# Weight remainders on VectorE during the scan's inverse, a rotation copy on GpSimd, and an order edge for the RWKV output

## The chip, the cores and the metric

The kernel runs on one core of one Trainium2 chip. The metric is the device time of one execution in microseconds (us). Engines are named as the profile names them: PE is TensorE's matmul and PEld its weight load, DVE is VectorE, ACT is ScalarE, POOL is GpSimd, SP is the engine that issues most DMAs. L265 is line 265 of the kernel before.

## The reference, cut to what matters

Two layers act on 512 latent and 256 context tokens of width 1024. Each layer normalises its input, projects it with one wide matrix, feeds three groups of heads, and projects their joint output back:

```python
p_l = split_projection(h @ w_in)          # latent, 4352 columns
p_c = split_projection(hc @ w_in)         # context
y_rwkv = rwkv_mixer(...)                  # 4 heads of 64, forward and backward in time
y_conv = short_conv_mixer(...)            # width 3
y_attn = diff_attention_mixer(...)        # 4 heads, rotary positions on q and k
x = x + gate * rms_norm(concat(y_rwkv, y_conv, y_attn) @ w_out, post_g)
```

RWKV is a recurrence, once per direction. The attention part rotates q and k of the latent tokens before the scores:

```python
S = S * w_t + (S @ a_t) b_t + v_t k_t;  y_t = S @ r_t
rotate: concat([x1 * cos - x2 * sin, x2 * cos + x1 * sin])
RWKV readout: y = group_norm(y_fwd + y_bwd) * ln_g + ln_b + bonus * v, times silu(z)
```

## The kernel before

**Numbers in two parts.** Most large matmuls run in a reduced-precision 32-bit format (F32R), so an operand is held as a rounded high part and a remainder ("low part"), and three products are summed: high by high, high of the weight by low of the activation, low of the weight by high of the activation. `split` (L247 to L269) does it for each 128x512 piece of a weight matrix: a DMA on SP's queue brings the raw piece (`wraw`, two buffers), ACT casts it (`whi`, L265), and one subtraction (`wlo`, L268) makes the low part. `whi` and `wlo` have three buffers each. The variable `eng` chooses who subtracts. A running count would alternate GpSimd and VectorE, but with `pool_only` the choice is always GpSimd, and the projections that fill the scan all pass `pool_only`.

**Filler.** The projections of the conv group, the gates, and attention's q, k and v are Python generators that emit a few matmuls at each step. `fill(us)` advances them by a number of microseconds of matmul work. They are spread through the RWKV scan, so that PE has independent work while the recurrence waits.

**The scan.** `rwkv_scan` handles the 768 tokens in three blocks b = 0, 1, 2 of 256 tokens for each direction d = 0, 1; a block has four chunks of 64 tokens. For a block, `rwkv_stage1` builds small matrices R (matmul `s`, masked by DVE), `rwkv_diag` collects diagonal blocks D, and `rwkv_inverse` inverts triangular matrices. The inverse begins with 28 dependent DVE steps on tiny operands (tiles `invt` and `Acc`, L118 in the profile since every DVE operation is recorded at the line of the wrapper `Vec`); between them the function `hook` emits filler. Four groups of small matmuls (`mg`) follow, each behind `fill` of 3 to 4 us. While a block is inverted, `adv` also advances `rwkv_prep` of the next block, which uses ACT, DVE and POOL (tiles `ld`, `Lc`, `E`, `Ei`, `km`, `x1`, `ar`, `bk`).

Then four steps p = 0 to 3 run one after the other, each a serial chain: PE `ch<-zu,R`; DVE copies to `gs`; PE `ch<-gs,XT`; two copies to `zu` on ACT (L968) and two on DVE; PE `ch<-zu,R` again; and DVE adds `pz`, which POOL (L947) made from the previous `zu`. The outputs `Y` are copied by ACT (L991) or added by DVE.

**Rotation of q and k.** For each of four heads h, `qk` in `attn_proj` projects q (i = 0) and k (i = 1). ACT evicts them from PSUM into `t` (tile `qkr`, L1118); four DMAs bring the half-swapped copy `sw` (tile `qks`, L1123). Then `sw` is multiplied by the sine on POOL (L1124), `t` by the cosine (L1125) and the two are added (L1126); the sum is cast into `sw` as the high part by ACT (L1127), the low part is `t` minus `sw` (L1128), and both go to DRAM. The three operations at L1125, L1126 and L1128 are on DVE for the heads in `QV = (2, 3)` and on POOL for heads 0 and 1.

**RWKV output.** `rwkv_out` normalises `Y`: in layer 0 first the four context chunks, then the eight latent chunks; in layer 1 the latent chunks alone. It loads v into `Vs`, and POOL multiplies it by the bonus and adds a bias (L1019, L1021). DVE reduces the means (`mu`), subtracts them, and computes a variance from ACT's squares (`gnsq`), a reciprocal root, two products and a sum. PE transposes the result (`yT`) and DVE multiplies it by the gate into `yr`. `Vs`, `gnsq` and the scan's `ar` share two buffers (tag `wk`).

**What sets the order.** Each engine runs its own queue in order. The queues are laid out at compile time by a list scheduler: it takes the program order as priority and places an instruction when its own model of the times says that it is ready. An edge of class `NoSync` given by `add_manual_dep` makes the scheduler place one instruction behind another without a semaphore. A wait that is longer on the chip than in the model holds everything behind it on that queue.

Of the kernel before, what the change touches and what calls it, by code (L numbers as in the profile page):

```python
# [11 lines left out]
F32R = mybir.dt.float32r  # L12
I32 = mybir.dt.int32
AF = mybir.ActivationFunctionType
ALU = mybir.AluOpType
AX = mybir.AxisListType
PSUM = bass.MemoryType.PSUM

P = 128
# [7 lines left out]
HD = 64  # L27
# [38 lines left out]
QV = (2,3)  # L66
# [40 lines left out]
def build(tc, A):  # L107
    nc = tc.nc
    ctx = ExitStack()
    S, G = nc.scalar, nc.gpsimd  # L110
# [17 lines left out]
    V = Vec()  # L128
# [63 lines left out]
    def small(n, tag, pool=None, bufs=2):  # L192
        return (pool or sm).tile([P, n], F32, tag=tag, bufs=bufs, name=tag)
# [55 lines left out]
    def split(src_ap, pool=wp, tag="w", out_tag=None, pool_only=False, nr=WR, nh=WH, out_pool=None):  # L249
        if lin.get("raw") and tag == "w":  # L250
            raw = lin["raw"].tile([P, 512], F32, tag="oraw", bufs=OB, name="wraw")
        else:
            raw = pool.tile([P, 512], F32, tag=tag + "raw", bufs=nr, name=tag + "raw")
        i = nc.sync.dma_start(out=raw, in_=src_ap)
        if lin.get("wafter"):
            tc.add_manual_dep(i.ins, lin["wafter"], mybir.DependencyInfo(
                mybir.DependencyClass.NoSync, mybir.DependencyReason.DATA), reason="order")
            lin["wafter"] = None
        if out_tag is None:
            hi = pool.tile([P, 512], F32R, tag=tag + "hi", bufs=nh, name=tag + "hi")  # L260
            lo = pool.tile([P, 512], F32R, tag=tag + "lo", bufs=nh, name=tag + "lo")
        else:
            hi = out_pool.tile([P, 512], F32R, name=out_tag + "hi")
            lo = out_pool.tile([P, 512], F32R, name=out_tag + "lo")
        S.copy(hi, raw)  # L265
        wcount[0] += 1
        eng = G if wcount[0] % 2 == (tag != "m") or pool_only else V
        eng.tensor_tensor(out=lo, in0=raw, in1=hi.bitcast(F32), op=ALU.subtract)  # L268
        return hi, lo  # L269

# [564 lines left out]
    def rwkv_scan(l, st, rw, lat, cx):  # L835
# [38 lines left out]
        for b in range(3):  # L874
# [21 lines left out]
            def adv(k):  # L896
                while pq and k:
                    try:
                        next(pq[0])
                        k -= 1  # L900
                    except StopIteration:
                        pq.pop(0)
# [8 lines left out]
            def hook(i):  # L911
                fill(F["i"] if b < 2 else F["i2"])
                if i >= H0 and i % HD_ == 0:
                    adv(1)

            rwkv_inverse(od, D, Bm, MS, I32, rw, XT, hook, adv)
            adv(AP)
            fill(F["m2"])
            for p in range(4):
# [19 lines left out]
                for d in range(2):  # L939
                    gs[d] = rw.tile([P, 2, HD], F32, tag="gs", bufs=2, name="gs")  # L940
                    cp = V.tensor_copy(gs[d], pv[d][:, 0])
                if not end:
                    for d in range(2):
                        pz[d] = rw.tile([P, 2, HD], F32, tag="pz", bufs=2, name="pz")
                        for h in range(2):
                            hr = slice(h * 64, h * 64 + 64)
                            G.tensor_tensor(out=pz[d][hr], in0=zu[d][hr, :, h, :],  # L947
                                            in1=prepd[d][1][hr, :, cc[d][1]].unsqueeze(2).to_broadcast([64, 2, HD]),
                                            op=ALU.mult)
# [49 lines left out]
    def rwkv_out(l, st, yr, rw):  # L999
        n = NL if l == L - 1 else NT  # L1000
        zr = rw.tile([P, 2, NT], F32, tag="kkn", name="zr")
        nc.sync.dma_start(out=zr[:, :, :n], in_=zrd[l].rearrange("a p t -> p a t")[:, :, :n])
        Y = st["Y"]
        lng = rw.tile([P, 2, 2, HD], F32, tag="lng", name="lng")
        for h in range(2):
            nc.scalar.dma_start(out=lng[h * 64:h * 64 + 64].rearrange("p a b v -> p (a b v)"),
                                in_=A["lngb"][l, h:h + 1, :].to_broadcast([64, 256]))
        for c0, nch in ((0, 8),) if l == L - 1 else ((8, 4), (0, 8)):
            nu = nch * 2
            Yu = Y[:, c0:c0 + nch].rearrange("p c a v -> p (c a) v")  # L1010
            bon = st["bon"][:, 2 * c0:2 * c0 + nu]
            Vs = rw.tile([P, 8, 2, HD], F32, tag="wk", bufs=WK, name="Vs")
            for h in range(2):
                for hp in range(2):
                    o = hp * P + h * 64
                    nc.sync.dma_start(out=Vs[h * 64:h * 64 + 64, 0:nch, hp, :],
                                      in_=vd[l][c0 * 64:(c0 + nch) * 64, o:o + 64].rearrange("(c t) v -> t c v", t=64))
            Vu = Vs[:, :nch].rearrange("p c a v -> p (c a) v")
            G.tensor_tensor(out=Vu, in0=Vu, in1=bon.unsqueeze(2).to_broadcast([P, nu, HD]), op=ALU.mult)  # L1019
            for hp in range(2):  # L1020
                G.tensor_tensor(out=Vs[:, :nch, hp], in0=Vs[:, :nch, hp],  # L1021
                                in1=lng[:, 1, hp].unsqueeze(1).to_broadcast([P, nch, HD]), op=ALU.add)
            mu = small(24, "mu")
            V.tensor_reduce(out=mu[:, :nu], in_=Yu, axis=AX.X, op=ALU.add)
            V.tensor_scalar_mul(mu[:, :nu], mu[:, :nu], -1.0 / HD)
            V.tensor_tensor(out=Yu, in0=Yu, in1=mu[:, :nu].unsqueeze(2).to_broadcast([P, nu, HD]), op=ALU.add)
            sq = rw.tile([P, 24, HD], F32, tag="wk", bufs=WK, name="gnsq")
            S.activation(sq[:, :nu], Yu, AF.Square)
            var = small(24, "var")
            V.tensor_reduce(out=var[:, :nu], in_=sq[:, :nu], axis=AX.X, op=ALU.add)  # L1030
            V.tensor_scalar(out=var[:, :nu], in0=var[:, :nu], scalar1=1.0 / HD, scalar2=GN_EPS,
                            op0=ALU.mult, op1=ALU.add)
            rs = small(24, "gnrs")
            rsqrt(var[:, :nu], nu, rs[:, :nu])
            V.tensor_tensor(out=Yu, in0=Yu, in1=rs[:, :nu].unsqueeze(2).to_broadcast([P, nu, HD]), op=ALU.mult)
            for hp in range(2):
                yh = Y[:, c0:c0 + nch, hp]
                V.tensor_tensor(out=yh, in0=yh, in1=lng[:, 0, hp].unsqueeze(1).to_broadcast([P, nch, HD]), op=ALU.mult)
                V.tensor_tensor(out=yh, in0=yh, in1=Vs[:, :nch, hp], op=ALU.add)
                fill(F["o"] if hp == 0 else F["o2"])  # L1040
                lin["next"] = MG & 64
                pb = psalt("yT")
                for c in range(nch):
                    for h in range(2):
                        hr = slice(h * 64, h * 64 + 64)
                        T.matmul(pb[hr, c * 64:c * 64 + 64], Y[hr, c0 + c, hp, :], ident[hr, hr], start=True, stop=True,
                                 tile_position=(h * 64, h * 64))
                n = nch * 64
                ts_ = slice(c0 * 64, c0 * 64 + n)
                V.tensor_tensor(out=yr[:, hp, ts_], in0=pb[:, :n], in1=zr[:, hp, ts_], op=ALU.mult)  # L1050
# [54 lines left out]
    def attn_proj(l, lat, cx):  # L1105
# [8 lines left out]
        def qk(h, fk=()):  # L1114
            for i in range(2):
                t, sw = fst("qkr"), fst("qks")
                yield from proj_ch(l, lat, cx if i else cxx,
                                   lambda o, c, nn: S.mul(t[:, c:c + nn], o, 1.0 if i else 0.125), fk=fk)  # L1118
                nn = NT if i else n
                for j in range(2):  # L1120
                    for x in range(2):
                        a, b = j * 64 + x * 32, j * 64 + 32 - x * 32
                        pin((S if SW else nc.sync).dma_start(out=sw[a:a + 32, :NL], in_=t[b:b + 32, :NL]), 2)  # L1123
                G.tensor_tensor(out=sw[:, :NL], in0=sw[:, :NL], in1=sinT, op=ALU.mult)  # L1124
                (V if h in QV else G).tensor_tensor(out=t[:, :NL], in0=t[:, :NL], in1=cosT, op=ALU.mult)  # L1125
                (V if h in QV else G).tensor_tensor(out=t[:, :NL], in0=t[:, :NL], in1=sw[:, :NL], op=ALU.add)  # L1126
                S.copy(sw[:, :nn].bitcast(F32R), t[:, :nn])  # L1127
                (V if h in QV else G).tensor_tensor(out=t[:, :nn].bitcast(F32R), in0=t[:, :nn], in1=sw[:, :nn], op=ALU.subtract)  # L1128
                pin((S if QQ else nc.sync).dma_start(out=qd[l][i, 0, h, :, :nn], in_=sw[:, :nn]), 1)
                pin(nc.sync.dma_start(out=qd[l][i, 1, h, :, :nn], in_=t[:, :nn]), 1)  # L1130
# [602 lines left out]
```

## Time and profile before

| | |
|---|---|
| median of 3 runs | 1142.31 us (1136.71, 1142.31, 1142.92) |
| the profiled execution | 1136.55 us |
| its span, first to last instruction | 1134.8 us |
| mean granted TensorE clock | 0.978 of full speed |
| DMA | 142.55 MB, mean 126 GB/s |

The profiled execution is 1.75 us longer than its span and lies 5.76 us (0.5%) below the median of the three runs. Busy times of the engines stand in the rows below. Times in the rows are microseconds from the start of the span. In a row of a timeline the columns are start, duration, engine, line, operation, output<-inputs with the shape, and a count when several like instructions are merged; a bracket gives how long the engine sat idle just before it and what ended the idle time.

### The profile page before, as it was taken

The numbers are of one execution on the slowest core, as the hardware profiler recorded it, in microseconds if no ns is written. First come the engines' busy times: TensorE is split into PE (matmuls) and PEld (weight loads), VectorE is DVE, ScalarE is ACT, GpSimd is POOL, SyncE is SP. The second block draws the span as 40 slices with busy tenths as digits, with TensorE's granted clock in tenths as the row PEclk, the third lists the DMA queues.
The fourth block names the chain that finished last, engine by engine and source line by source line (L and its number), as shares of the span: only waits on it lengthen the run. The fifth ranks groups of instructions, "written<-read, shape, count | busy, mean of one in ns | idle before, by whom it ended". The sixth has DMA issues, their size and how long they took to land.

```text
span 1134.8 us, 25347 instructions
## 1 busy us (share of the span) xinstructions
PE 1029.8 (91%) x9850; PEld 844.0 (74%) x9850; DVE 714.8 (63%) x1736; ACT 523.7 (46%) x1330; POOL 446.5 (39%) x452
## 2 busy tenths in 40 slices
PE   4899989999699998989899899998988999888897
PEld 1577968777588867878787786876767897777775
DVE  3530558788467262489847857776985824579944
ACT  3432553453363223478724564654353532248731
POOL 0311534434736522432222345255475454431322
PEclk9999999999999999989999999999998999999999
DMA  9574322212334466654052452232223345546143
GB/s 354 178 242 134 86 79 57 58 35 71 133 85 130 131 192 194 201 172 103 15 190 85 139 180 86 70 96 71 78 79 103 99 127 160 165 149 183 48 158 111
DMA packets 92088, 142.55 MB, mean 126 GB/s; under 512 B 28192, under 2 KB 36416, under 8 KB 91968
## 3 DMA queue, kind: packets, MB, share of 16 engines
q1 hardware_dynamic: 88512, 136.14, 39.0%
q10 hardware_dynamic: 3456, 4.80, 1.3%
q8 instruction: 77, 1.26, 0.5%
q14 instruction: 43, 0.35, 0.1%
HBM read 110.99 MB, written 25.71 MB: 120 GB/s over the span
## 4 chain that ended last, share of the span: by engine, by line
PE 41%; DVE 15%; ACT 7%; issue 6%; POOL 6%; DMA 3%; SPq 1%; ACTq 0%; DVEq 0%; POOLq 0%
PE pcl L137 14%; PE op L137 6%; PE ptl L137 3%; PE pcc L137 3%; PE av L137 2%; PE ptc L137 2%; PE sc L137 2%; DVE mx L118 2%; PE ch L135 1%; DMA mraw<-in_mod_w_dram 1%; ACT e L1250 1%; DVE bk L118 1%; DVE rs_t L118 1%; PE yps L135 1%; POOL wlo L268 1%
## 5 line engine op out<-in xcount | busy, mean ns | idle before, releaser
L268 POOL TENSOR_TENSOR wlo<-wraw,whi 128x512 fp32r<-128x512 f32 x134 | 181.6, 1358 | 303.1 <-ACT whi L265 261.6
L137 PE MATMUL pcl<-lat,whi 128*128 128x512 f32 (+1 forms) x928 | 294.6, 394 | 2.6 <-issue 1.6
L137 PEld LDWEIGHTS pcl<-lat,whi 128*128 128x128 f32 x928 | 169.8, 190 | 40.0 <-issue 7.5
L137 PE MATMUL pcl<-lat,wlo 128*128 128x512 f32 (+1 forms) x464 | 184.6, 398 | 2.9 <-POOL wlo L268 2.9
L265 ACT CAST whi<-wraw 128x512 fp32r<-128x512 f32 x144 | 88.8, 619 | 149.6 <-DMA wraw<-in_w_in_dram 38.7
L137 PE MATMUL pcc<-ctx,whi 128*128 128x256 f32 x576 | 111.4, 290 | 2.2 <-DVE ctx L118 1.7
L137 PEld LDWEIGHTS pcl<-lat,wlo 128*128 128x128 f32 x464 | 87.8, 189 | 27.1 <-issue 4.5
L137 PEld LDWEIGHTS pcc<-ctx,whi 128*128 128x128 f32 x576 | 94.0, 195 | 9.2 <-issue 3.2
L137 PE MATMUL pcc<-ctx,wlo 128*128 128x256 f32 x288 | 83.7, 291 | 2.0 <-DVE wlo L118 2.0
L137 PE MATMUL ptl<-whi,lat 128*128 128x256 f32 x384 | 79.2, 293 | 0.0
L1250 ACT ACTIVATE e<-sc,mx 128x768 f32<-128x768 f32 (+1 forms) x80 | 66.3, 831 | 15.9 <-DVE mx L118 10.4
L118 DVE TENSOR_REDUCE mx<-sc 128x1 f32<-128x768 f32 (+1 forms) x72 | 63.9, 921 | 14.7 <-PE sc L137 14.7
L137 PE MATMUL av<-vA,aT 128*128 128x128 f32 x416 | 58.7, 285 | 10.1 <-ACT aT L1285 10.0
L137 PEld LDWEIGHTS av<-vA,aT 128*128 128x128 f32 x416 | 54.2, 194 | 16.0 <-ACT aT L1285 12.9
L137 PEld LDWEIGHTS ptl<-whi,lat 128*128 128x128 f32 x384 | 63.1, 195 | 2.0 <-issue 0.5
L118 DVE TENSOR_TENSOR R<-s,cs 128x384 f32<-128x384 f32 (+1 forms) x96 | 47.0, 530 | 19.6 <-PE s L135 18.9
L137 PEld LDWEIGHTS pcc<-ctx,wlo 128*128 128x128 f32 x288 | 55.9, 194 | 4.6 <-DVE wlo L118 2.2
L137 PE MATMUL sc<-KH,QS 128*128 128x256 f32 (+1 forms) x144 | 52.8, 380 | 4.5 <-ACT e L1250 2.9
L947 POOL TENSOR_TENSOR pz<-zu,pc 64x128 f32<-64x128 f32 x88 | 39.5, 449 | 43.2 <-DVE zu L118 38.5
L137 PE MATMUL ptl<-wlo,lat 128*128 128x256 f32 x192 | 56.1, 292 | 0.0
L137 PE MATMUL sc<-KL,QS 128*128 128x256 f32 (+1 forms) x144 | 46.3, 342 | 0.0
L118 DVE COPY zu<-ch 64x128 f32<-64x128 f32 x48 | 14.1, 294 | 47.8 <-ACT zu L968 41.8
(448 smaller groups left out, 2403.6 us busy)
## 6 DMA issues: line engine op xcount, KB each, us to landing
wraw<-in_w_in_dram SPq DMA_DIRECT2D x144, 256.0 KB, 2.7
mraw<-in_mod_w_dram SPq DMA_DIRECT2D x96, 256.0 KB, 4.5
KH<-qd SPq DMA_DIRECT2D x32, 192.0 KB, 3.8
oraw<-in_w_out_dram SPq DMA_DIRECT2D x20, 256.0 KB, 3.6
qd<-qks SPq DMA_DIRECT2D x12, 384.0 KB, 2.3
qd<-qkr SPq DMA_DIRECT2D x12, 384.0 KB, 2.5
qks<-qkr SPq DMA_DIRECT2D x64, 64.0 KB, 2.1
zu<-vd SPq DMA_DIRECT2D x96, 32.0 KB, 2.2
```

The source lines that it names most:

```text
L118: i = f(*a, **k)
L135: tc.keep_in_program_order(nc.tensor.matmul(*a, **k))
L137: i = nc.tensor.matmul(*a, **k)
L265: S.copy(hi, raw)
L268: eng.tensor_tensor(out=lo, in0=raw, in1=hi.bitcast(F32), op=ALU.subtract)
L947: G.tensor_tensor(out=pz[d][hr], in0=zu[d][hr, :, h, :], in1=prepd[d][1][hr, :, cc[d][1]].unsqueeze(2).to_broadcast([64, 2, HD]), op=ALU.mult)
L1250: ac(S.activation(ej[:, c], pb[:, c], AF.Exp, bias=mx[:, i:i + 1], accum_out=den[:, u["h"] * 6 + tt, j:j + 1]))
```

## The change

Three edits. The first sets a flag while `rwkv_inverse` is emitted; `split` then chooses VectorE for the low part of the weights that are taken there, the matmul filler's. The second has GpSimd instead of ScalarE make the rotated high part for heads 0 and 1, in both layers: eight copies, six of 128x768 and two of 128x512. The third remembers, in block b = 2, the last `gs` copy of step p = 0, and places two instructions of each group of `rwkv_out` behind it by a `NoSync` edge: the first product on `Vs` (POOL) and the first reduction `mu` (DVE).

```diff
@@ split
-        eng = G if wcount[0] % 2 == (tag != "m") or pool_only else V
+        eng = G if (wcount[0] % 2 == (tag != "m") or pool_only) and not lin.get("scan") else V
@@ rwkv_scan
+            lin["scan"] = True
             rwkv_inverse(od, D, Bm, MS, I32, rw, XT, hook, adv)
+            lin["scan"] = False
...
                     cp = V.tensor_copy(gs[d], pv[d][:, 0])
+                if b == 2 and p == 0:
+                    st["step"] = cp.ins.name
@@ rwkv_out
+        def behind(i):
+            tc.add_manual_dep(i.ins, st["step"], mybir.DependencyInfo(
+                mybir.DependencyClass.NoSync, mybir.DependencyReason.DATA), reason="order")
...
-            G.tensor_tensor(out=Vu, in0=Vu, in1=bon.unsqueeze(2).to_broadcast([P, nu, HD]), op=ALU.mult)
+            i = G.tensor_tensor(out=Vu, in0=Vu, in1=bon.unsqueeze(2).to_broadcast([P, nu, HD]), op=ALU.mult)
...
+            behind(i)
             mu = small(24, "mu")
-            V.tensor_reduce(out=mu[:, :nu], in_=Yu, axis=AX.X, op=ALU.add)
+            i = V.tensor_reduce(out=mu[:, :nu], in_=Yu, axis=AX.X, op=ALU.add)
+            behind(i)
@@ attn_proj, qk
-                S.copy(sw[:, :nn].bitcast(F32R), t[:, :nn])
+                (S.copy if h in QV else G.tensor_copy)(sw[:, :nn].bitcast(F32R), t[:, :nn])
```

## Rows read from the trace of the kernel before

**Rows 1.** From the page: the busy time of each engine with its share of the span and its instructions, and the chain of work that ended last, by engine.

```profile
PE 1029.8 (91%) x9850; PEld 844.0 (74%) x9850; DVE 714.8 (63%) x1736; ACT 523.7 (46%) x1330; POOL 446.5 (39%) x452
...
PE 41%; DVE 15%; ACT 7%; issue 6%; POOL 6%; DMA 3%; SPq 1%; ACTq 0%; DVEq 0%; POOLq 0%
```

**Rows 2.** The waits of one engine for another over the whole span: total us, times, longest us.

```profile
POOL wlo L268 <- ACT whi L265: 261.6, 72, 22.5
DVE zu L118 <- ACT zu L968: 41.8, 36, 7.4
...
ACT qks L1127 <- POOL qkr L1126: 34.0, 7, 7.5
...
DVE wlo L118 <- ACT whi L265: 14.6, 6, 4.4
```

**Rows 3.** TensorE's timeline at two places in block b = 1, in layer 0 and in layer 1.

```profile
301.36 0.63 PE L135 MATMUL ch<-gs,XT 64*64 64x64 f32 x16
...
309.15 0.37 PE L137 MATMUL ch<-zu,R 128*64 128x64 f32 x1 [5.55 <-DVE zu L118]
...
863.80 0.37 PE L137 MATMUL yps<-zu,rt 64*64 64x64 f32 x1 [4.15 <-ACT Y L991]
```

**Rows 4.** Busy time by stretch: the two gaps of rows 3, each with the stretch right behind it. The columns are the stretch, its length, busy us (instructions) of PE, PEld, DVE, ACT and POOL, the granted clock, the DMA share and GB/s.

```profile
303.60:309.10 5.50, 0.00 (x1) 0.00 (x0) 0.59 (x2) 1.87 (x4) 4.48 (x4) 0.76 0.49 162
309.10:313.30 4.20, 4.15 (x50) 3.81 (x52) 2.79 (x6) 0.54 (x2) 3.45 (x6) 0.50 0.66 217
859.60:863.80 4.20, 0.05 (x1) 0.00 (x1) 1.15 (x3) 1.05 (x3) 3.87 (x6) 0.89 0.02 3
863.80:869.70 5.90, 5.90 (x66) 5.56 (x68) 0.59 (x2) 1.16 (x4) 3.77 (x4) 0.50 0.42 152
```

**Rows 5.** ScalarE's timeline at the same two places.

```profile
306.52 0.83 ACT L1127 CAST qks<-qkr 128x768 fp32r<-128x768 f32 x1 [6.71 <-POOL qkr L1126]
...
307.89 0.26 ACT L968 COPY zu<-ch 64x128 f32<-64x128 f32 x1
...
862.75 0.83 ACT L1127 CAST qks<-qkr 128x768 fp32r<-128x768 f32 x1 [7.46 <-POOL qkr L1126]
863.49 0.43 ACT L991 COPY Y<-yps 128x128 f32<-128x128 f32 x2
```

**Rows 6.** GpSimd's timeline around the gap of layer 0.

```profile
305.22 1.26 POOL L1126 TENSOR_TENSOR qkr<-qkr,qks 128x512 f32<-128x512 f32 x1
307.43 1.80 POOL L1128 TENSOR_TENSOR qkr<-qkr,qks 128x768 fp32r<-128x768 f32 x1 [0.94 <-ACT qks L1127]
309.19 1.27 POOL L268 TENSOR_TENSOR wlo<-wraw,whi 128x512 fp32r<-128x512 f32 x1
310.98 2.50 POOL L947 TENSOR_TENSOR pz<-zu,pc 64x128 f32<-64x128 f32 x4 [0.52 <-DVE zu L118]
```

**Rows 7.** GpSimd's timeline around the gap of layer 1.

```profile
861.46 1.26 POOL L1126 TENSOR_TENSOR qkr<-qkr,qks 128x512 f32<-128x512 f32 x1
862.68 0.87 POOL L947 TENSOR_TENSOR pz<-zu,pc 64x128 f32<-64x128 f32 x2
863.73 1.81 POOL L1128 TENSOR_TENSOR qkr<-qkr,qks 128x768 fp32r<-128x768 f32 x1 [0.18 <-ACT qks L1127]
865.49 0.87 POOL L947 TENSOR_TENSOR pz<-zu,pc 64x128 f32<-64x128 f32 x2
```

**Rows 8.** Groups of instructions by line and shape: busy us, mean ns of one, idle time before them. The last row is of the view of the tile `wlo` and gives shortest, median and longest ns, and the first and last start.

```profile
L268 POOL TENSOR_TENSOR wlo<-wraw,whi 128x512 fp32r<-128x512 f32 x134 | 181.6, 1358 | 303.1 <-ACT whi L265 261.6 <-PE pcl L137 12.7 <-DMA wraw<-in_w_in_dram 9.8
L1180 POOL MEMSET KL<- 64x768 f32 x16 | 11.9, 743 | 39.9 <-PE sc L137 28.6 <-PE yps L135 11.0
L1128 POOL TENSOR_TENSOR qkr<-qkr,qks 128x768 fp32r<-128x768 f32 x6 | 11.0, 1832 | 4.0 <-ACT qks L1127 4.0
...
L118 DVE TENSOR_TENSOR wlo<-wraw,whi x10: 679/693/694, 26.8 to 652.6; 128x512 fp32r<-128x512 f32 x10
```

**Rows 9.** The sum over the instructions of the tile `wlo` in six stretches, one about each inverse (174 to 211, 253 to 300, 342 to 382, 727 to 766, 806 to 852, 893 to 932): busy time of each engine, and the mean of a stretch.

```profile
sum 248.00, PE 124.59 PEld 71.96 DVE 0.00 POOL 64.03; mean PE 20.76 PEld 11.99 DVE 0.00 POOL 10.67
```

**Rows 10.** Inside the inverse of block 1, layer 0: VectorE's timeline, and GpSimd's over the same time.

```profile
264.08 0.25 DVE L118 TENSOR_TENSOR Acc<-Acc,invt 128x88 f32<-128x88 f32 x1
...
264.64 1.27 DVE L118 TENSOR_TENSOR Acc<-Acc,invt 128x72 f32<-128x72 f32 x1
...
264.52 2.78 POOL L268 TENSOR_TENSOR wlo<-wraw,whi 128x512 fp32r<-128x512 f32 x2 [5.61 <-ACT whi L265]
```

**Rows 11.** VectorE's timeline: the first instruction behind the 28 steps that needs PE, in block 2 of layer 0 and in block 1 of layer 1.

```profile
367.63 0.42 DVE L118 TENSOR_TENSOR MS<-mg,I 128x256 f32<-128x256 f32 x1 [4.76 <-PE mg L135]
...
831.04 0.41 DVE L118 TENSOR_TENSOR MS<-mg,I 128x256 f32<-128x256 f32 x1
```

**Rows 12.** TensorE's gaps behind it in block 1: layer 0, then layer 1.

```profile
294.13 0.21 PE L137 MATMUL mg<-T,ms 32*32 32x32 f32 x1 [1.96 <-ACT ms L818]
...
838.66 0.48 PE L137 MATMUL lora<-lora,lup 64*128 64x256 f32 x1 [1.56 <-DVE T L118]
```

**Rows 13.** The RWKV output: the first reduction of layer 0's context group, its variance, and the busy time in steps 0 to 3 of block 2 in layer 0 (columns as in rows 4).

```profile
247.56 0.68 DVE L118 TENSOR_REDUCE mu<-Y 128x8 f32<-128x512 f32 x1
...
347.21 0.68 DVE L118 TENSOR_REDUCE var<-gnsq 128x8 f32<-128x512 f32 x1
...
385.20:409.80 24.60, 24.60 (x350) 18.44 (x354) 10.69 (x38) 5.76 (x15) 8.50 (x13) 1.00 0.49 142
```

## The prediction

> **What bounds the kernel now.** Begin with the page: PE is busy for 91% of the span and has 41% of the chain that ended last, more than any other engine [rows 1]. PE's work is the same after the change, so an edit pays only where it closes one of PE's gaps, and the next view is PE's timeline. Its two largest gaps inside the scan are alike: 5.55 us before `ch<-zu,R` at 309.15 in layer 0, and 4.15 us before `yps<-zu,rt` at 863.80 in layer 1, both in block 1 [rows 3]. The reader should follow each to its cause. In layer 0, PE had finished `ch<-gs,XT` by 302.0 [rows 3], and the copies that consume it are ACT's and DVE's. ACT started its copy only at 307.89, because the rotation's cast (L1127) stood in front of it on ACT's queue and had kept ACT idle for 6.71 us until POOL finished the addition at L1126 [rows 5]. In layer 1 the same cast held ACT for 7.46 us, and the copy of Y that PE's next output buffer needed came right behind it [rows 5]. The list of waits shows this as a class: seven waits of this cast on POOL, 34.0 us, and it also counts 41.8 us of DVE waiting for ACT's `zu` copies [rows 2]. The stretches behind the gaps are slow as well: PE, idle just before, is granted 0.50 of its clock (the 1.2 GHz level) for 4.2 us and for 5.9 us, while it is busy for 4.15 and 5.90 us of them [rows 4].
>
> **Edit two, the copy on GpSimd.** It takes the cast out of ACT's queue for heads 0 and 1, eight casts in all, and both gaps stand behind one of them. The value of layer 0's: 5.55 us of gap, and half of the 4.15 us that PE ran at half clock, 2.1 us, together 7.65 us. Of layer 1's: 4.15 and half of 5.90, 2.95, together 7.1 us. The sum is 14.75 us. I count the clock with the gap because in both places the lower level follows the gap.
>
> What POOL pays is not in the trace: a copy of 128x768 into F32R. From below, a memset of 64x768 took 0.743 us; from above, the two-input subtraction of 128x768 into F32R took 1.832 us [rows 8]. I take 1.3 us, the middle, since a copy reads one input where the one reads none and the other two.
>
> Now what is late next. POOL's queue carries `pz` of the coming step behind the rotation. In layer 0 POOL ends L1126 at 306.48, would copy until 307.78, subtract (L1128, 1.80) until 309.58, make a `wlo` (1.27) until 310.85 and then `pz` [rows 6], which is 0.13 us before today's start. The scan wants it some 7.65 us earlier than today, and the queue is in order. But in this inverse POOL also loses `wlo` work ahead of this point (below), at least one of 1.3 us and perhaps three, so I charge 1.0 us of new wait (bounds 0 and 2.5, the whole `pz` row). In layer 1 there is less room: L1126 ends at 862.72, half of `pz` at 863.55, the copy at 864.85, L1128 (1.81) at 866.66 and the other half of `pz` (0.87) at 867.5 [rows 7]. Today PE needs about 5.9 us from `yps` to the addition that uses `pz`, nearly all at half clock; at full clock I estimate 4.4 us, which from the gap's start at 859.65 is 864.0. So `pz` would be 3.5 us late (0 if the scheduler puts it in front, 4.15 if it takes the gap's whole place). Net for edit two: 14.75 - 1.0 - 3.5 = 10.25 us. The stores of the high part on SP's queue wait for the copy instead of the cast: its end moves from 307.35 to 307.78 and from 863.58 to 864.85, so loads behind them start 0.4 and 1.3 us later; those weights are one piece ahead of PE, and I cost this at nothing. If that cover is gone it costs the same 0.4 and 1.3.
>
> **Edit one, weights on VectorE.** The stretches around the six inverses hold 64.03 us of POOL's `wlo` [rows 9], at a mean of 1.358 us [rows 8]: 47 pieces, about eight to an inverse. On DVE one takes 0.693 us [rows 8], so DVE gains 47 x 0.693 = 32.6 us. It gets something back: while POOL subtracts, a step of the inverse that takes 0.25 us takes 1.27 [rows 10], a loss of 1.02. If each piece costs one such stall today, DVE ends 0.33 us better a piece; if none does, 0.69 worse. I take two stalls for three pieces, which cancels the cost: zero. Off the path is what happens in block 2: DVE ends its steps early and then waits 4.76 us for PE [rows 11], enough for most of eight pieces at 0.69 us, 5.5. In block 1 of both layers there is no such wait: the same instruction in layer 1 has no idle time before it [rows 11], and PE has gaps behind, 1.96 and 1.56 us [rows 12]. There eight pieces at -0.33 to +0.69 make -2.6 to +5.5 us an inverse, -5 to +11 for two. The new wait: DVE's `wlo` needs ACT's `whi`, and the 28 dependent steps and later the next block's preparation queue behind it. The ten pieces that DVE already makes waited six times, 14.6 us [rows 2], 2.4 us each, where DVE had nothing else to do; POOL waited 261.6 us at the same point [rows 2], unharmed. The bounds of that are 0 and 2.4 us a wait. A wait once taken aligns the next pieces, so I keep zero for the edit.
>
> The Trainium skill, "GPSIMD Engine Reference", section "Key points", says that GpSimd shares its SBUF interfaces with VectorE and contends with VectorE instructions that have two SBUF inputs. Rows 10 agree, and the rule speaks for edit one but against edit two, whose copies would hold VectorE in turn. By it alone the two copies at the gaps could add their 1.3 us each, and the sum would be 2.6 us higher. Nothing below uses this.
>
> **Edit three, the output ordered later.** In layer 0 the context group's reductions leave the time before and inside the inverses of blocks 1 and 2, where `mu` (0.68) and the variance (0.68) now run [rows 13]. By these the group is six passes of about 0.68 and a dozen tiny operations of at most 0.25, some 7 us. Behind the new edge it meets steps 0 to 3 of block 2, where DVE is busy for 10.69 of 24.6 us [rows 13]: 13.9 idle us hide it. Its removal from the inverse of block 2 gains nothing, because DVE waits for PE there anyway [rows 11]. POOL's products on `Vs` move with it; its load is not pinned, though the later group's load waits for a shared buffer. I cost this at zero, with bounds -1.4 (the two reductions, were they on the path) and +7 (PE at `yT`, were the cover gone).
>
> **The sum.** 1136.55 - 10.25 + 0 + 0 = 1126.3 us against the profiled execution. That one is 5.76 us below the median; of the four executions shown two lie near 1136.6 and two near 1142.6, and their mean is 1139.6. From it the sum is 1129.4, and I predict 1129.5.
>
> **Rivals.** (a) GpSimd becomes the wait: `pz` is late by the upper bounds in both layers and PE's clock falls behind the remaining gap in layer 1. Then layer 0 gives 7.65 - 2.5 = 5.1, layer 1 7.1 - 4.15 - 2.95 = 0, and the time is 1134.5. For it: POOL is busy 4.48 of 5.50 and 3.87 of 4.20 us in the two gaps [rows 4]. Against: pieces leave POOL. (b) More than forecast: `pz` is on time and the two gaps of rows 12 go too, as the POOL work that shares their time goes: 14.75 + 3.5 = 18.3, 1121.3. For it, rows 10; against it, rows 7. (c) Slower: DVE's queue in block 1. No stall is recovered, eight pieces add 5.5 us to each of the two inverses without slack, and each has two waits for `whi` at 2.4 us: 11 + 9.7 = 20.7 against 10.25, so +10.4 and 1150. It decides once the two together lose more than 10.25 us. For it: the missing idle time in rows 11; against: rows 10, and ACT freed of its longest waits. The change doing less than it says is part of (a): the copy leaves ACT for certain.
>
> **How the numbers follow.** Forecast 0.47, (a) 0.22, (b) 0.13, (c) 0.18. About 0.5%, 5.7 us, is what a measurement can tell from no change here. The forecast and (b) are faster; (a) at -5.1 is mostly the same, 0.05 of it faster; of (c) 0.03 is too weak to see. So faster 0.65, same 0.20, slower 0.15. The range runs from 1116, (b) with some of block 1's -5, to 1147, short of all of (c): its pure form is left out. The likeliest case's own range is 1123 to 1135.
>
> **What would show it.** Right: no `qks` cast of heads 0 and 1 on ACT, no wait of it on `qkr` L1126 but for other heads; the gaps of 5.55 and 4.15 us gone or under 4 and their stretches at full clock; some 47 `wlo` on DVE; inverse steps of 1.27 us gone. The copy shows as a POOL group of 0.75 to 1.83 us. Wrong: gaps before `ch<-zu,R` that end on POOL `pz`; a DVE `wlo` idle on `whi` inside the inverse with PE gaps before `mg`; PE waiting at `yT`; or new gaps of several us where none of the three edits acts, from another order of the queues.

## The result, and the profile after

The changed kernel takes 1131.85 us (median of 14 runs, 1127.51 to 1143.27), the kernel before beside it 1141.38 us (14 runs, 1132.22 to 1149.74). The ratio is 0.9937 with a 95% interval of 0.9909 to 0.9965: faster, by some 7 us (4 to 10 by the interval), and the time lies inside the predicted range. The ratios leave disturbed runs of either kernel out, so they are not quite the quotients of the medians. The profiled execution took 1133.62 us (span 1131.8, mean granted clock 0.982), against 1136.55 us before: in these two executions the gain is only 2.9 us, which will matter below.

The page of the change: busy time by engine, and the two groups that make the weights' low parts.

```profile
PE 1028.5 (91%) x9850; PEld 841.9 (74%) x9850; DVE 730.9 (65%) x1789; ACT 519.1 (46%) x1322; POOL 386.1 (34%) x407
...
L268 POOL TENSOR_TENSOR wlo<-wraw,whi 128x512 fp32r<-128x512 f32 x81 | 109.1, 1351 | 208.4 <-ACT whi L265 195.3
...
L118 DVE TENSOR_TENSOR wlo<-wraw,whi 128x512 fp32r<-128x512 f32 x63 | 47.1, 753 | 47.6 <-ACT whi L265 47.1
```

POOL made 134 low parts before [rows 8] and makes 81 now, so 53 moved. POOL lost 60 us of work and DVE gained 16 [rows 1]; PE's work is the same.

TensorE's timeline of the change, at the largest gaps of block 1 in layer 0 (the first two rows) and in layer 1:

```profile
307.60 0.68 PE L135 MATMUL ch<-gs,XT 64*64 64x64 f32 x16 [1.59 <-DVE gs L118]
...
310.32 0.27 PE L137 MATMUL ch<-zu,R 128*64 128x64 f32 x1 [0.42 <-DVE zu L118]
...
840.93 0.21 PE L137 MATMUL mg<-T,ms 32*32 32x32 f32 x1 [2.45 <-ACT ms L818]
...
863.49 0.37 PE L137 MATMUL ch<-zu,R 128*64 128x64 f32 x1 [4.43 <-DVE zu L118]
```

Against [rows 3]: layer 0's 5.55 us are 1.59. Layer 1's 4.15 us before `yps` are gone, but 4.43 us stand in the same step, before its second `ch<-zu,R`. The 2.45 us before `mg<-T,ms` are new in layer 1. To see what holds the 4.43 us, read ScalarE's queue and then GpSimd's at the same time:

```profile
859.95 0.26 ACT L972 COPY zu<-ch 64x128 f32<-64x128 f32 x1 [4.77 <-POOL pz L951]
862.66 0.26 ACT L972 COPY zu<-ch 64x128 f32<-64x128 f32 x1 [2.45 <-POOL pz L951]
```

```profile
857.38 1.29 POOL L1137 TENSOR_TENSOR qkr<-qkr,qks 128x512 f32<-128x512 f32 x1
858.74 0.82 POOL L1138 CAST qks<-qkr 128x768 fp32r<-128x768 f32 x1
859.52 0.40 POOL L951 TENSOR_TENSOR pz<-zu,pc 64x128 f32<-64x128 f32 x1
859.88 1.79 POOL L1139 TENSOR_TENSOR qkr<-qkr,qks 128x768 fp32r<-128x768 f32 x1
861.76 1.35 POOL L951 TENSOR_TENSOR pz<-zu,pc 64x128 f32<-64x128 f32 x3
```

`pz` reads the old `zu`, and ACT's copy (L972, L968 before) writes into that same tile. So the copy itself, and not only DVE's later addition, has to wait until `pz` is done, and `pz` stands behind the rotation in GpSimd's queue. The last `pz` ends at 863.11, PE starts at 863.49.

The stretches of the change, columns as in [rows 4]. First, in layer 0, the one with the gap of 1.59 us and the one behind it, both at the full clock, where [rows 4] had 0.50 behind the gap. Then the inverse of block 2 in layer 0, the gap of layer 1, and the stretch behind that, which is at the lower clock (0.50, the 1.2 GHz level) as before.

```profile
306.01:310.30 4.29, 2.31 (x29) 2.03 (x28) 2.10 (x5) 1.04 (x3) 3.70 (x6) 1.00 0.48 168
310.30:314.50 4.20, 4.18 (x75) 3.55 (x77) 3.01 (x9) 0.50 (x2) 3.01 (x5) 1.00 0.72 213
...
337.90:347.10 9.20, 9.20 (x80) 8.22 (x77) 7.90 (x31) 2.25 (x6) 0.39 (x2) 1.00 0.20 54
859.06:863.49 4.43, 0.00 (x0) 0.00 (x1) 0.59 (x2) 0.52 (x2) 4.12 (x7) 0.85 0.44 177
862.18:869.01 6.83, 5.52 (x60) 4.63 (x60) 3.84 (x10) 1.17 (x5) 3.80 (x7) 0.50 0.43 131
```

### The profile page after: what moved, and what is told of

The parts are those of the page before. It is cut to its first block, busy times and chain, and to the rows that moved or that the text cites. A ratio compares the mean times of both kernels' runs of the same rounds, so it can differ in the third digit from the quotient of the medians.

```text
span 1131.8 us, 25323 instructions
## 1 busy us (share of the span) xinstructions
PE 1028.5 (91%) x9850; PEld 841.9 (74%) x9850; DVE 730.9 (65%) x1789; ACT 519.1 (46%) x1322; POOL 386.1 (34%) x407
## 3 DMA queue, kind: packets, MB, share of 16 engines
q8 instruction: 77, 1.26, 0.5%
## 5 line engine op out<-in xcount | busy, mean ns | idle before, releaser
L268 POOL TENSOR_TENSOR wlo<-wraw,whi 128x512 fp32r<-128x512 f32 x81 | 109.1, 1351 | 208.4 <-ACT whi L265 195.3
L118 DVE TENSOR_TENSOR wlo<-wraw,whi 128x512 fp32r<-128x512 f32 x63 | 47.1, 753 | 47.6 <-ACT whi L265 47.1
L137 PE MATMUL av<-vA,aT 128*128 128x128 f32 x416 | 57.9, 282 | 10.6 <-ACT aT L1296 10.5
L118 DVE TENSOR_TENSOR R<-s,cs 128x384 f32<-128x384 f32 (+1 forms) x96 | 47.1, 530 | 18.3 <-PE s L135 17.5
L1135 POOL TENSOR_TENSOR qks<-qks,sinT 128x512 f32<-128x512 f32 x16 | 22.5, 1405 | 84.2 <-DMA qks<-qkr 71.8
```

Of the source, the lines that this page charges most:

```text
L118: i = f(*a, **k)
L137: i = nc.tensor.matmul(*a, **k)
```

## The experiments

Each has its own profile and is timed beside the kernel before on the same chip. All ratios are to the kernel before. First the parts, as a table, since they are read against each other. The three pairs were timed together, and so were the three single parts, each group beside its own runs of the kernel before.

| edits in the kernel | ratio, 95% interval | median us (runs) |
|---|---|---|
| one, two, three (the change) | 0.9937 [0.9909, 0.9965] | 1131.85 (14) |
| two and three | 0.9941 [0.9902, 0.9980] | 1137.50 (8) |
| one and three | 0.9913 [0.9879, 0.9946] | 1134.99 (6) |
| one and two | 0.9899 [0.9870, 0.9929] | 1132.79 (6) |
| two alone | 1.0027 [0.9996, 1.0058] | 1142.41 (12) |
| one alone | 0.9978 [0.9943, 1.0013] | 1140.39 (12) |
| three alone | 0.9997 [0.9961, 1.0033] | 1140.63 (12) |

**One part taken away.**

```diff
@@ two and three: split
-        eng = G if (wcount[0] % 2 == (tag != "m") or pool_only) and not lin.get("scan") else V
+        eng = G if (wcount[0] % 2 == (tag != "m") or pool_only) else V
@@ one and three: qk
-                (S.copy if h in QV else G.tensor_copy)(sw[:, :nn].bitcast(F32R), t[:, :nn])
+                S.copy(sw[:, :nn].bitcast(F32R), t[:, :nn])
@@ one and two: rwkv_out
         def behind(i):
+            return
```

> Edits two and three without edit one: all low parts on GpSimd again. Theory (the copy carries the gain, edit one is worth about nothing on the path): 5 to 10 us faster than the kernel before, as the full change was (9.5 by the medians); the gap before ch<-zu,R in block 1 of layer 0 stays under 3 us, and ACT's copies of zu wait for POOL's pz up to 3 us longer than in the changed kernel. Rival (edit one carries it, by freeing GpSimd in the inverse): within 3 us of the kernel before, with gaps of 4 us or more in block 1 of both layers that end on pz behind the rotation.

> Edits one and three without edit two: ACT casts the rotated q and k of all heads again. Theory: within 3 us of the kernel before; ACT idle for 4 to 8 us at a time before the cast of heads 0 and 1, and PE gaps over 3 us before ch or yps in block 1 of both layers. Rival (edit one carries the gain): 6 to 10 us faster than before, because GpSimd reaches the addition in front of the cast earlier and the two gaps fall below 2 us.

> Edits one and two without the order edge. Theory (edit three is worth nothing on the path): within 2.5 us of the changed kernel; the context group's mu and variance run again before and inside the inverses of blocks 1 and 2, and DVE still waits 3 us or more for PE at MS in block 2. Rival (the edge keeps DVE free where the change has filled it): 4 us or more slower than the changed kernel, with the wait at MS in block 2 of layer 0 gone and a PE gap before mg there.

Each pair keeps the gain within the intervals. The surprise is the pair without edit two. ScalarE's cast waits for GpSimd again, and both old gaps are back, only smaller:

```profile
310.48 0.27 PE L137 MATMUL ch<-zu,R 128*64 128x64 f32 x1 [4.27 <-DVE zu L118]
...
864.16 0.36 PE L137 MATMUL yps<-zu,rt 64*64 64x64 f32 x1 [3.10 <-ACT Y L995]
```

Still this kernel is at 0.9913. So the gain is not the closing of these two gaps alone, and the next idea was that edits one and two stand in for each other.

The pair without edit three keeps all of edit two, and in layer 1 it does what the prediction hoped. PE reaches `ch<-gs,XT` at 856.78 as in the change (856.75), but the four DMAs that bring the half-swapped copy are issued from 844.98 on instead of 847.42, GpSimd begins the rotation at 850.54 instead of 854.20, and the last `pz` ends at 859.68 instead of 863.11:

```profile
858.33 1.35 POOL L951 TENSOR_TENSOR pz<-zu,pc 64x128 f32<-64x128 f32 x3
```

```profile
860.05 0.27 PE L137 MATMUL ch<-zu,R 128*64 128x64 f32 x1 [0.96 <-DVE zu L118]
```

```profile
860.05:866.00 5.95, 5.73 (x99) 4.84 (x101) 4.38 (x12) 2.61 (x11) 2.70 (x5) 1.00 0.33 85
```

So 0.96 us of gap stand there for the change's 4.43, with the full clock behind. Between these two profiles, what edit two brings in layer 1 hangs on when the rotation meets this step. (Before `mg<-T,ms` the pair pays 3.53 us, for the change's 2.45.) The pair of edits two and three, whose layer 0 gap is closed as well, has 5.43 us there.

**One part alone**, with a fourth kernel that has edits one and two and `pz` of block 1 on VectorE.

> Edit two alone: heads 0 and 1 have their high part copied on GpSimd, everything else as in the kernel before. Theory (edits one and two are two ways to the same time: both shorten GpSimd's or ScalarE's queue in front of the scan's zu copies, and the order edge is worth nothing): a ratio of 0.991 to 0.996, about 5 to 10 us faster, close to the run that left only the weights out (0.994); layer 0's gap before ch<-zu,R is under 2 us, layer 1's stays at 4 to 6 us, now behind pz. Rival A (the sum of parts: edit two carries what the whole change gains and edit one none): 0.990 to 0.993, as the best of the runs so far. Rival B (any new order of the queues gains, because the kernel before is a poor draw): also faster, and then the order edge alone is faster too.

> Edit one alone: the weight remainders that fall into the inverse go to VectorE, everything else as in the kernel before. Theory (substitutes): 0.989 to 0.995, as the run without the copy (0.991); the gap before ch<-zu,R in layer 0 is still 3 to 5 us, because ScalarE's cast still waits for GpSimd, but steps of the inverse of over 1 us are gone and the scans end earlier. Rival A (edit one is worth nothing, as it was costed): 0.998 to 1.003. Rival B (any new order gains): faster, but the order edge alone as well.

> Edit three alone: the RWKV output's reductions and products are held behind step 0 of block 2, everything else as in the kernel before. Theory: within 3 us of the kernel before (0.997 to 1.003), and both large gaps of block 1 (before ch<-zu,R in layer 0, before yps in layer 1) still there. Rival B (any new order of the queues gains): 0.995 or less. Rival C (the edge costs): 1.003 or more, with TensorE waiting at yT.

That idea fell: no part alone is faster beyond its interval, and edit two alone leans to the slow side. Rival B (any new order gains) falls too. The group of runs in which the single parts were timed does show gains: the fourth kernel in it is at 0.9922. So the parts need each other, and the profile of edit two alone shows one place where they do. Layer 0's gap of block 1 is closed here too (1.38 us are left), and layer 1's is 5.43; but there is a gap that no other kernel has, in layer 0's inverse of block 2:

```profile
366.50 0.20 PE L137 MATMUL mg<-T,Bm 32*32 32x16 f32 x1 [5.48 <-DVE T L118]
```

VectorE and GpSimd ahead of it, still with edit two alone (each step was about 0.25 us in [rows 10]):

```profile
360.45 1.18 DVE L118 TENSOR_TENSOR invt<-Acc 128x52 f32<-128x52 f32 x1
361.67 1.19 DVE L118 TENSOR_TENSOR Acc<-Acc,invt 128x52 f32<-128x52 f32 x1
362.89 1.16 DVE L118 TENSOR_TENSOR invt<-Acc 128x28 f32<-128x28 f32 x1
364.08 1.21 DVE L118 TENSOR_TENSOR Acc<-Acc,invt 128x28 f32<-128x28 f32 x1
```

```profile
360.29 1.27 POOL L268 TENSOR_TENSOR wlo<-wraw,whi 128x512 fp32r<-128x512 f32 x1
361.52 1.25 POOL L1031 TENSOR_TENSOR Vs<-Vs,lng 128x512 f32<-128x512 f32 x1
362.75 1.26 POOL L268 TENSOR_TENSOR wlo<-wraw,whi 128x512 fp32r<-128x512 f32 x1
363.96 1.26 POOL L1031 TENSOR_TENSOR Vs<-Vs,lng 128x512 f32<-128x512 f32 x1
```

One step of the inverse passes for each instruction of GpSimd, and it ends within 0.1 us of that instruction. The Trainium skill's "GPSIMD Engine Reference", section "Key points", has the two engines share their SBUF interfaces and contend where VectorE reads two SBUF inputs or runs in a 2-port perf mode. By the first half of that rule, the trace agrees: these are steps with two SBUF inputs. The length of this inverse goes with two things, how many instructions VectorE runs in it (28 are the steps, the others weights or parts of the RWKV output) and how long GpSimd is busy beside them. The four rows are that stretch with edit two alone, in the kernel before, with edits two and three, and with edits one and two:

```profile
340.50:365.30 24.80, 20.52 (x135) 18.42 (x133) 24.44 (x47) 5.60 (x12) 19.55 (x17) 0.97 0.44 126
```

```profile
345.10:360.90 15.80, 15.80 (x83) 13.67 (x82) 15.49 (x46) 3.92 (x8) 8.48 (x8) 0.93 0.43 117
```

```profile
343.70:355.60 11.90, 11.90 (x74) 10.36 (x72) 10.90 (x28) 2.98 (x7) 5.58 (x7) 1.00 0.33 96
```

```profile
340.90:355.80 14.90, 14.90 (x93) 13.10 (x91) 14.64 (x49) 3.55 (x8) 5.19 (x7) 1.00 0.42 107
```

In the kernel before, the last two steps take 0.20 and 0.21 us, at 360.48 and 360.72, inside the pause of 0.95 us in which GpSimd waits for ScalarE's cast. With the copy on GpSimd and nothing else moved, GpSimd runs on without that pause, and into this one inverse fall weights, a whole rotation and the output's products on `Vs`: 19.55 us. The inverse grows from 15.8 to 24.8 us and PE runs dry. Either of the other edits takes enough of GpSimd's work away (5.58 and 5.19 us are left), and PE is busy throughout; edit three also takes the output's steps out of VectorE's queue (28 instructions for 46). Edit one alone fits, with 49 instructions, 4.28 us of GpSimd and 14.3 us, and so does edit three alone, with 28, 1.66 and 8.9. That this one place accounts for the whole difference between edit two alone and the pairs is not shown.

> Edits one and two, without the order edge, and pz of block 1 on VectorE: a version that leaves out the part that has shown no gain and takes layer 1's wait for GpSimd's pz away. Theory (gaps count one for one): 2 to 5 us faster than the run without the order edge, a ratio of 0.986 to 0.989. Rival (the gap in layer 1 is paid back elsewhere, as with pz on VectorE and the edge kept): the same as the run without the edge, 0.989 to 0.992, with the gap before mg<-T,ms still at some 3.5 us.

```diff
-                            G.tensor_tensor(out=pz[d][hr], in0=zu[d][hr, :, h, :],
+                            (V if b == 1 else G).tensor_tensor(out=pz[d][hr], in0=zu[d][hr, :, h, :],
```

It came out at 0.9922 [0.9889, 0.9955], beside the rival's upper end, with 2.44 us before `mg<-T,ms` and 3.45 us before `ch<-zu,R` in layer 1. An earlier run had the same edit on the full change:

> The whole change, and in block 1 the product pz is made by VectorE instead of GpSimd. Theory (the gap left in layer 1, 4.43 us before ch<-zu,R, is ACT's and DVE's zu copies waiting for pz, which stands behind the rotation in GpSimd's queue): that gap falls under 1.5 us, the half-clock stretch behind it goes, layer 0's 1.59 us goes too or is unchanged, and the time is 4 to 8 us below the changed kernel's. Rival (the gap hangs on something else that is late at the same time, DVE's bk products or the next v rows): it stays over 3 us, and VectorE's extra 32 products make the time the same or up to 5 us more.

0.9913 [0.9876, 0.9949], not told apart from the change. VectorE's timeline of this run has the reason; the first row is the step of the gap, the second the next step:

```profile
856.25 3.76 DVE L118 TENSOR_TENSOR pz<-zu,pc 64x128 f32<-64x128 f32 x4
...
863.77 1.20 DVE L118 TENSOR_TENSOR pz<-zu,pc 64x128 f32<-64x128 f32 x4
```

Beside the rotation four `pz` take 3.76 us on VectorE instead of 1.20. The queue is left, the contention is not: the gap shrinks from 4.43 to 2.43 us, between the theory's 1.5 and the rival's 3.

**The cast on VectorE.**

```diff
-                (S.copy if h in QV else G.tensor_copy)(sw[:, :nn].bitcast(F32R), t[:, :nn])
+                (S.copy if h in QV else V.tensor_copy)(sw[:, :nn].bitcast(F32R), t[:, :nn])
```

> The change, with the high part of rotated q and k of heads 0 and 1 copied on VectorE instead of GpSimd. Theory (any engine that makes the scan's copies pays for a wait on GpSimd's rotation in its own queue): VectorE now waits for L1137 as ScalarE did, 3 to 6 us at a time, gaps of 3 us and more come back before ch<-zu,R or ch<-gs,XT in block 1 of both layers, and the time is 3 to 8 us longer than the change: a ratio of 0.997 to 1.003. Rival (only ScalarE's queue was the trouble, and GpSimd was short of time): VectorE's copy is short and idle time hides it, pz comes 1 us earlier, and the ratio is 0.988 to 0.993.

0.9980 [0.9947, 1.0012]: by the ratio most of the gain is gone, as the theory said, though the interval overlaps the change's. The wait has moved to VectorE's queue, 26.1 us in seven waits for L1137, and 3.29 us of gap before `ch<-gs,XT` come back in layer 0, behind this one:

```profile
304.79 0.56 DVE L118 CAST qks<-qkr 128x768 fp32r<-128x768 f32 x1 [4.52 <-POOL qkr L1137]
```

In layer 1 no gap of that kind over 3 us came back; its 3.52 us before `mg<-T,ms` are of the kind that the kernels with edit one have (2.33 to 3.53).

**Edit one left out in one inverse.**

```diff
-            lin["scan"] = True
+            lin["scan"] = (l, b) != (1, 1)
```

> The change, but in one of the six inverses, that of block 1 in layer 1, the weight remainders stay shared between GpSimd and VectorE as in the kernel before. Theory (edit one costs there what it gives elsewhere: VectorE's queue has no room, the pieces push the scan of decays Lc into GpSimd's rotation): the gap of 2.45 us before mg<-T,ms falls under 1 us, one to four steps of that inverse take 1.27 us again and cost nothing, and the kernel is 2 to 4 us faster than the change, a ratio of 0.989 to 0.992. Rival (GpSimd's pieces put the rotation and with it pz later): the gap before ch<-zu,R in layer 1 grows to 5 us and more, as in the run without any of the weights, and the ratio is 0.993 to 0.997.

The gap before `mg<-T,ms` falls from 2.45 to 0.29 us, as the theory expected, and the 4.43 us before `ch<-zu,R` stay. But the time is 0.9933 [0.9902, 0.9964], the change's own, and not the theory's 0.989 to 0.992. What this gap is worth is too small to be seen here.

**The gaps filled.** Does the lower clock belong to a gap? Products that are thrown away keep TensorE busy through it:

```diff
@@ the kernel before; the second loop stands ahead of the copies to gs
+                for k in range(100 if (l, b, p) == (0, 1, 0) else 0):
+                    T.matmul(pv[0][0:64, 0, 0, :], XT[0][0:64, cc[0][1] * 2, :], gs[0][0:64, 0, :],
+                             start=True, stop=True, tail=True)
+                for k in range(80 if (l, b, p) == (1, 1, 1) else 0):
+                    T.matmul(pv[0][0:64, 1, 0, :], R[0][:, 0, 0, 0, :], zu[0][:, 0, 0, :],
+                             start=True, stop=True, tail=True)
@@ the change has the first loop, with 90 if (l, b, p) == (1, 1, 1)
```

> The kernel before, with products that are computed twice and thrown away: 100 matmuls of 64x64 behind ch<-gs,XT of the first step of block 1 in layer 0, and 80 of 128x64 ahead of yps<-zu,rt of the second step of block 1 in layer 1, so that TensorE is busy through most of the two gaps of 5.55 and 4.15 us while the waits for GpSimd stay. Theory (the lower clock behind a gap is part of the gap's price, as the prediction counted it): TensorE keeps its full clock behind both, the waits are as long as before, and the time falls by up to the two halves counted, 2.1 and 2.95, together some 5 us: a ratio of 0.994 to 0.998, with a mean granted clock above the 0.974 of before. Rival (the clock falls at these places whether or not TensorE is busy there, or falls elsewhere in its stead): 0.999 to 1.004, and the mean clock as before.

> The change, with 90 matmuls of 64x64 computed twice and thrown away behind ch<-gs,XT of the second step of block 1 in layer 1, where the change has 4.43 us of gap and then 6.83 us at half clock. Theory: ScalarE still waits for pz, the gap is under 1.5 us, the clock behind it is full, and the kernel is some 3 us faster than the change: a ratio of 0.988 to 0.992. Rival: the same as the change, 0.992 to 0.996.

Both are slower than expected: 1.0067 [1.0036, 1.0099] and 0.9991 [0.9956, 1.0027]. The filler was too long. In the second kernel its 90 products and the 16 records of the regular ones took

```profile
851.96 11.18 PE L135 MATMUL ch<-gs,XT 64*64 64x64 f32 x196 [1.39 <-DVE gs L118]
```

where the regular ones alone take 0.68, so some 10.5 us stand in for a gap of 4.43, and ScalarE's copies now waited for TensorE. So their times don't price the clock. The mean granted clock of the first kernel speaks for the theory, 0.9808 (12 runs) against 0.9746 in the kernel before beside it (29): of the spans, 22.1 us in place of 29.0 are lost to the lower clock, 6.9 less, where the prediction counted 5.05 for the two places. As to where the clock falls the profiles speak too: the stretch with the filler and the one behind it, in layer 0 of the first kernel and in layer 1 of the second,

```profile
299.20:311.60 12.40, 12.40 (x199) 12.20 (x199) 0.59 (x2) 1.87 (x4) 6.53 (x5) 1.00 0.51 170
311.60:317.50 5.90, 5.90 (x103) 5.42 (x103) 3.57 (x9) 1.03 (x5) 2.27 (x4) 1.00 0.27 69
```

```profile
851.90:864.70 12.80, 12.74 (x209) 12.54 (x209) 0.60 (x3) 0.52 (x2) 4.76 (x7) 1.00 0.25 91
864.70:870.60 5.90, 5.68 (x100) 4.79 (x101) 4.34 (x12) 2.56 (x11) 1.73 (x4) 1.00 0.12 26
```

are at the full level, where the unfilled gaps of these two places had 0.50 behind them ([rows 4], and 862.18:869.01 of the change). The first kernel's other filler, in layer 1, is at the full level from 860 to 878 as well. At these places the lower clock does follow the idle time.

## Why the prediction was right or wrong

The time and the direction were right: 1129.5 was said, 1131.85 came. The gain was smaller than its sum, some 7 us by the ratio for 10.25, and the sum was only partly right; that the time came so near is in part luck.

**Edit two, layer 0: right.** Of 7.65 us less 1.0, 6.65, the profile shows 5.55 - 1.59 = 3.96 us of gap and the 2.1 us at the lower clock, which is not granted there any more: 6.1. The new wait that was charged at 1.0 us costs PE 0.42. What is left, 1.59, is another wait: two `bk` products of DVE that took 3.40 us together beside GpSimd's rotation:

```profile
303.63 3.40 DVE L118 TENSOR_TENSOR bk<-km,Ei 64x512 f32<-64x512 f32 x2
```

**Edit two, layer 1: wrong.** 7.1 us less 3.5 were counted, 3.6. Nothing came: 4.43 us of gap for 4.15, and the lower clock is still there. The failed step is the one that let `pz` be wanted at 864.0, by the addition. It is wanted first by the copies into `zu`, as soon as `ch<-gs,XT` is done, some 857.4 in this profile, since they overwrite what `pz` reads. With that demand the prediction's own queue, copy and low part ahead of half of `pz`, gives rival (a)'s price for layer 1, a net of 0. The same queue with the rotation 3.66 us earlier, in the run without the order edge, leaves 0.96 us: the two profiles differ in the time at which the rotation meets the step, and the prediction took that time as it was before. The copy itself was well sized: 0.82 to 1.29 us, median 1.05, for 1.3.

**Edit one: its value was wrong by its company.** Costed at zero as if alone, it is within measurement of that alone, 0.9978 [0.9943, 1.0013]. What the prediction missed is that it makes edit two pay, as edit three does in its stead: in the inverse of block 2 above it takes weights out of a GpSimd that the copy had made denser. Of its terms, 53 pieces for 47 and 47.1 / 21 = 2.2 us a wait for 2.4 were close. "Two stalls for three pieces" was too many: in four pairs of kernels with and without the edit DVE's busy time grows by 20.6 (710.3 to 730.9), 19.3 (706.5 to 725.8), 19.0 (714.8 to 733.8) and 14.7 us (722.9 to 737.6, from two alone to one and two), 0.28 to 0.39 a piece; a piece takes 0.693, so 0.30 to 0.42 us, of a stall of 1.02, comes back: about one for three pieces. Stretched steps did go, as forecast: the longest of the 168 in six inverses took 1.88 us before and 0.56 after. Block 1 of layer 1 paid with the new 2.45 us, and the clock from 840.90 to 844.50, behind that gap, is 0.61.

**Edit three: right alone, wrong as cover.** 0.9997 [0.9961, 1.0033] is the zero that was costed, and its reductions now stand at 377.73, in the first step of block 2, and the largest gap of PE from 376 to 404, its four steps, is 0.65 us. But beside edit two without edit one it takes the products on `Vs`, and VectorE's output steps, out of the crowded inverse: two alone is 1.0027, two and three 0.9941.

**Rival (c)** did not come about: DVE's 21 waits for `whi` did not hold PE enough to show. **Rival (a)** was true for layer 1 and false for layer 0.

**What carries the total.** The two profiled executions differ by 2.9 us, the medians by 9.5. Of before, 32 runs timed beside the single parts have a mean span of 1139.3 us at a mean granted clock of 0.9748, those of the change 1130.9 at 0.9795. Span times clock, the time that it would be at full clock, is 1110.6 (standard error 0.5) and 1107.7 (0.6): 2.9 us of the 8.4 are there, and (1 - 0.9748) x 1139.3 - (1 - 0.9795) x 1130.9 = 5.5 us are clock. This is bookkeeping and no cause, but it says that most of the gain is fewer stretches at half clock, of which the prediction counted 5.05 us, in two places. Only layer 0's 2.1 was seen there. One more stretch shows in the rows above: the inverse of block 2 in layer 0 was granted 0.93 in the kernel before and 1.00 in the change. Where the rest of the clock came from is open. Two of the pairs gain by the clock alone: span times clock is 1109.7 for two and three and 1109.5 for one and three, against 1109.8 for the kernel before beside them (standard errors 0.7 to 0.8). How one and three does that (mean clock 0.9788, against 0.9733) with both old gaps at 4.27 and 3.10 us is open. A total that came true on terms that partly did not is worth less than it looks.

No kernel tried was told apart from the change on the fast side; one and two without the order edge has the lowest ratio, 0.9899, and its interval overlaps the change's.

## What to carry to other kernels

Where VectorE's steps end with GpSimd's instructions, as here (1.2 us for 0.25), the two engines are one resource: before an operation is moved to GpSimd, add up what GpSimd does in each stretch where VectorE has a serial chain, since the copy alone gained nothing until something else left that stretch. For a moved or delayed operation look for its earliest consumer, and an instruction that overwrites its input is one. A part that shows nothing alone may still be the one that lets another part pay, so take parts away one at a time before any of them is dropped.

## What was not expected of the hardware

A one-input instruction was held as well. In the change's block 1 of layer 1 a one-input copy of 128x8 from SBUF to SBUF took 1.26 us and ended with the GpSimd product that began just before it, and the two scans behind it, which read two inputs, took 3.27 us beside the next ones. VectorE, then GpSimd:

```profile
835.06 1.26 DVE L118 COPY ar<-kkn 128x8 f32<-128x8 f32 x1
...
836.68 3.27 DVE L118 TENSOR_TENSOR_SCAN Lc<-cs,ld 128x256 f32<-128x256 f32 x2
```

```profile
835.02 1.27 POOL L1135 TENSOR_TENSOR qks<-qks,sinT 128x512 f32<-128x512 f32 x1 [4.90 <-DMA qks<-qkr]
836.25 1.54 POOL L1136 TENSOR_TENSOR qkr<-qkr,cosT 128x512 f32<-128x512 f32 x1
```

In the kernel with the cast on VectorE, a copy of this form took 0.17 us at 290.51 and the two scans 1.27, with GpSimd idle. Whether VectorE ran the copy in a 2-port perf mode, the second half of the rule cited above, no run here shows. The copies to `gs`, which read PSUM, took 0.49 us for two at 307.06, while GpSimd made a low part from 306.43 to 308.15: those were not held.
